# A decoder trunk of two layers: attention as one pipeline of sixteen units, fewer convolution steps in the row split, and another order of the closing sums

## The chip, the cores and the metric

The kernel runs on one core of a Trainium2 chip. The metric is the device time of one execution in microseconds (us), the median of several. The core has these engines, each with its own instruction queue: PE (TensorE, matrix products; PEld is its loading of weights, which overlaps), DVE (VectorE), ACT (ScalarE), POOL (GpSimd) and SP (SyncE, which issues most DMA transfers here). Engines wait for each other through semaphores.

## The reference

512 tokens of width 1024 go through two layers. Layer A has a causal convolution module and a feed-forward network (FFN); then keys and values are projected once; layer B has sliding-window attention over them and another FFN; a last RMSNorm follows.

```python
h = h + conformer_conv(rmsnorm(h, norm_mix[0]), ...)   # pw1 -> GLU -> 31 taps per channel -> LayerNorm -> SiLU -> pw2
h = h + swiglu_ffn(rmsnorm(h, norm_ffn[0]), ffn_w_up[0], ffn_w_down[0])
k, v = split(rmsnorm(h, norm_kv) @ w_kv)               # 4 KV heads of 64
q = rmsnorm(h, norm_mix[1]) @ w_q                      # 16 heads of 64
h = h + banded_sink_attention(q, k, v, sinks, rel_bias) @ w_o
h = h + swiglu_ffn(rmsnorm(h, norm_ffn[1]), ffn_w_up[1], ffn_w_down[1])
out = rmsnorm(h, norm_final)

def banded_sink_attention(...):   # query block n of 128 sees key blocks n-1 and n, window 128
    s = q @ k_band * HEAD_DIM ** -0.5 + bias           # bias by distance; outside the window -1e30
    m = maximum(max(s), sink)
    p = exp(s - m)
    o = p / (sum(p) + exp(sink - m)) @ v_band

def swiglu_ffn(x, w_up, w_down):  # 1024 -> 2 x 2816 -> 1024
    gate, up = split(x @ w_up)
    return (silu(gate) * up) @ w_down
```

## The kernel before

**Layout.** Activations lie transposed: h is eight tiles ("rows" below) of 128 channels by 512 tokens, so each product takes a weight tile of 128x128 and streams tokens past it. Weights come as chunks of 512 KB in a fixed order. For each chunk `get` loads six chunks ahead and splits three ahead into a high part (ACT, L203) and a low part (DVE, L204); a product is then three matmuls in a reduced float32 format: high by high (L262), high by the activation's low part (L263), low by high (L264). Activations are split likewise into pairs (`quad` tiles). Four PSUM banks take one group of output rows.

**Layer A in halves.** The convolution is done for tokens 0 to 255 first (`h0`), then 256 to 511 (`h1`). A tap of the depthwise convolution is one DVE operation (L609, L611), or one ACT product (L601, L603) with a POOL addition (L604); L615 joins the two sums, and L649 is PE's sums over channels for the LayerNorm. The second half's convolution is a generator (`second`) of small steps. `job` gives it points (chunk, steps owed by then), and `pace`, called by every `get`, runs it to the straight line between two points. It runs beside the second pointwise product of the first half (pw2, eight chunks) and the FFN's first part of that half.

**The row split.** After each group of four rows of pw2 the rows of h are added (L731, DVE), scaled by ACT (L382), given their low part by DVE (L383), squared by ACT (L336) and summed by DVE (L340). The FFN's first product takes all eight rows one after the other.

**Attention.** The q product has two groups g of four chunks each. `q_evac` scales a group (L909) and splits it. A unit (gp, jp, n) is four heads of one 128-query block: twelve score matmuls (L928), six each into two banks, whose operands lie in the upper and the lower 64 rows of the array; L931 adds the bias and takes the maximum (DVE, four); exp is L938 (ACT, four); the reciprocal is L940; POOL scales by it (L942, four); L950 transposes on PE; L953 (ACT) and L954 (DVE) split the result into pth and ptl; then come the matmuls with v, and L968 (ACT) and L969 (DVE) split the unit's output. `pipeline(gp)` runs the eight units of a gp, each stage some units apart, in twelve steps. The first one steps beside the chunks of the second q group and is drained before the first o chunk; the second steps beside the first four o chunks and is drained after them. In the first unit of a gp (n = 0, two of eight) the scores are 128 wide in L931, in the others 256.

**The end.** The last FFN part is multiplied out for tokens 0 to 255 (`fa`), then for 256 to 511 (`fb`). Each row of h is added (L1047), squared (ACT, L1051) and the squares of the first five rows of fb (all eight of fa) are summed by POOL (L1053). `total` (L1039) has PE sum over channels; ms (L1070, DVE), rs (L1072, POOL), diag (L1074, DVE) and `spread` (L1084, and L1088 for fb) bring the reciprocal root to all partitions. Then the rows are scaled and stored: six tiles of each half by DVE (L1106), two by ACT and POOL (L1100). `fill` puts DVE products of fa into fb's chain, behind the instruction it names.

What sets the order: the program is written as above, but a scheduler with a timeline model of its own then puts each engine's instructions in order.

Of the kernel before, what the change touches and what calls it, by code (L numbers as in the profile page):

```python
# [21 lines left out]
KT = D // P  # L22
# [127 lines left out]
def hybrid_trunk(ctx: ExitStack, tc: tile.TileContext, xT, W, prm_in, wdw_in, sinks, relb, onehot, outT):  # L150
# [251 lines left out]
        return w == 512 or m % 2 == 1  # L402


    def down_group(keys, act_of, banks, on_step=None):
        nk = len(keys)
        w = banks[0].shape[-1]
        for ci, (key, kts) in enumerate(keys):
            whi, wlo = get(*key)
            order = [(k, m) for k in range(2) for m in range(4)]  # L410
            if ci == nk - 1:
                order = [(k, m) for m in range(4) for k in range(2)]
            for k, m in order:
                sl = slice(m * P, (m + 1) * P)
                mm3(banks[m], (whi[:, k, sl], wlo and wlo[:, k, sl]), act_of(kts + k),
                    ci == 0 and k == 0 and opens(m, w), ci == nk - 1 and k == 1 and closes(m, w))
                if on_step is not None and ci < nk - 1 and m == 3:
                    on_step()
            if on_step is not None and ci == nk - 1:
                on_step()  # L420
                on_step()

# [125 lines left out]
    with tc.tile_pool(name="conv", bufs=2) as cv:  # L548
# [272 lines left out]
            late.gate()  # L821
        h1.after = [h0.silu]
        base = seen[0]
        job(second, (base, 0), (base + 8, 20), (base + 36, h1.n_steps - early))
        x0 = {"ffn0": Act(KT)}
        bc0 = new_bc()
        n0 = Next(("ffn0",), x0, bc0, HALF[0], nc.vector)
# [31 lines left out]
    if True:  # L859
# [42 lines left out]
        qs = [None, None]  # L902
        os_ = [None, None]

        def q_evac(g, banks):
            qs[g] = (quad(), quad())
            for m in range(4):
                t = temp()
                nc.vector.scalar_tensor_tensor(t, banks[m], -HD ** -0.5, rs_bc, op0=ALU.mult, op1=ALU.mult)  # L909
                split((qs[g][0][:, m, :], qs[g][1][:, m, :]), t)  # L910
# [58 lines left out]
            nc.vector.tensor_sub(lo, src, f32(hi))  # L969
            yield  # L970

        def pipeline(gp):
            units = [unit(gp, jp, n) for n in range(NBLK) for jp in range(2)]
            done = 0
            for t in range(len(units) + 4):
                for d in (4, 3, 1, 0):
                    if 0 <= t - d < len(units):
                        next(units[t - d])
                        if d == 1:
                            next(units[t - d])  # L980
                yield

        def drain(it):
            for _ in it:
# [3 lines left out]
        banks = [bank() for _ in range(4)]  # L988
        down_group([(("q", kp, 0), 2 * kp) for kp in range(4)], lambda kt: xq[kt], banks)
        q_evac(0, banks)  # L990
        p0 = pipeline(0)
        banks = [bank() for _ in range(4)]
        down_group([(("q", kp, 1), 2 * kp) for kp in range(4)], lambda kt: xq[kt], banks,
                   on_step=lambda: next(p0, None))
        q_evac(1, banks)
        drain(p0)
        p1 = pipeline(1)
        nxt = Next(("ffn1",))
        for part in range(2):
            for g in range(2):  # L1000
                banks = [bank() for _ in range(4)]
                down_group([(("o", part * 2 + kp, g), 2 * kp) for kp in range(2)],
                           lambda kt: (os_[part][0][:, kt, :], os_[part][1][:, kt, :]), banks,
                           on_step=(lambda: next(p1, None)) if part == 0 else None)
                for m in range(4):
                    i = g * 4 + m
                    nc.vector.tensor_add(h[i], banks[m], h[i])
                    if part == 1:
                        nxt.on_h(i)
            if part == 0:  # L1010
                drain(p1)

    attn.close()
    ffn_part(1, 0, nxt.x["ffn1"], ALL, nxt.rms)
# [5 lines left out]
    class Fin:  # L1020
        def __init__(self, hf):
            self.hf, self.tok = hf, HALF[hf]
            self.banks, self.hg = [bank() for _ in range(4)], []
            self.n_pool = 2

        def down(self, kp, g):
            whi, wlo = get("down", 1, kp, g)
# [14 lines left out]
        def rows(self, g, other=lambda n, ins: None):  # L1042

            n_add = 5 if self.hf else KT
            for i in range(g * 4, g * 4 + 4):
                t = h[i][:, self.tok]
                add = nc.vector.tensor_add(t, self.banks[i // 2][:, (i % 2) * 256:(i % 2) * 256 + 256], t)  # L1047
                if i == KT - 1:
                    other(2, add.ins)
                sq = res.tile([P, 256], F32, tag="sq", name=uid("sq"), bufs=5)  # L1050
                self.squared = nc.scalar.square(sq, t).ins  # L1051
                if 0 < i < n_add:
                    nc.gpsimd.tensor_add(sq, self.acc, sq)  # L1053
                if i < n_add:
                    self.run = self.acc = sq
                if not self.hf or i < n_add:
                    continue
                if i == n_add:
                    self.st = bank()
                self.total(sq, i == n_add, i == KT - 1)  # L1060
                if i == KT - 2:
                    self.total(self.run, False, False)

        def sums(self, other=lambda n, ins: None):
            if not self.hf:
                self.st = bank()
                self.total(self.acc, True, True)
            st = self.st
            ms = small.tile([P, 4], F32, tag="ms", name=uid("ms"))
            other(2, nc.vector.tensor_scalar(ms[:, 0:2], st[:, 0:2], 1.0 / D, EPS, op0=ALU.mult, op1=ALU.add).ins)  # L1070
            rs = small.tile([P, 4], F32, tag="rs", name=uid("rs"))
            nc.gpsimd.tensor_tensor(rs[:, 0:2], ms[:, 0:2], mhalf[:, 0:2], op=ALU.pow)  # L1072
            self.diag = temp()[:, 0:256]
            other(2, nc.vector.tensor_mul(self.diag.rearrange("p (n q) -> p n q", n=2),  # L1074
                                          ident.unsqueeze(1).to_broadcast([P, 2, P]),
                                          rs[:, 0:2].unsqueeze(2).to_broadcast([P, 2, P])).ins)
            for i in range(self.n_pool):
                t = res.tile([P, 256], F32, tag="res", name=uid("res"))
                nc.scalar.mul(t, h[i][:, self.tok], col("fin", i))
                self.hg.append(t)  # L1080

        def spread(self):
            self.pb = bank()[:, 0:256]
            nc.tensor.matmul(self.pb, ones_m, self.diag, start=True, stop=True)  # L1084
            if self.hf:

                pb = bank()[:, 0:256]
                nc.tensor.matmul(pb, ones_m, self.diag, start=True, stop=True)  # L1088
                self.copy(pb)

        def copy(self, pb):
            self.bc = temp()[:, 0:256]
            nc.scalar.copy(self.bc, pb)

        def store(self, i, t, q=nc.sync):
            q.dma_start(outT[i][:, self.tok], t)
# [1 line left out]
        def out_pool(self):  # L1098
            for i, t in enumerate(self.hg):
                nc.gpsimd.tensor_mul(t, t, self.bc)  # L1100
                self.store(i, t, nc.scalar if self.hf else nc.sync)

        def out_dve(self):
            for i in range(self.n_pool, KT):
# [3 lines left out]
                self.store(i, t)  # L1108
                yield

    res = ctx.enter_context(tc.tile_pool(name="res", bufs=8))
    steps = [(kp, g) for kp in range(*LAST) for g in range(2)]
    fa = Fin(0)
    for kp, g in steps:
# [11 lines left out]
    for n, (kp, g) in enumerate(steps):  # L1126
# [5 lines left out]
            fa.spread()  # L1132
        elif n == 3:
            fb.rows(1, fill)
    with tc.issue_after(fb.squared):
        fa.copy(fa.pb)
    fa.out_pool()
    fb.sums(fill)
    fb.spread()
    for _ in fb.out_dve():  # L1140
# [28 lines left out]
```

## Time and profile before

| what | value |
|---|---|
| median of 3 runs | 1115.81 us (1115.38 to 1116.58) |
| the profiled execution | 1115.77 us |
| its span | 1114.0 us |
| mean PE clock | 0.993 of full |
| bytes moved by DMA | 125.00 MB, mean 112 GB/s |
| ACT busy, POOL busy | 502.6 us, 322.1 us |

A row of the timeline has the start, the duration, the engine, the line of the kernel, the operation, output and inputs, and how many instructions it stands for; in brackets follow the idle time before it and what ended that. Matmuls overlap, so what one costs is read from start to start. A row of a group has the total busy time and the mean in ns.

### The profile page before, as it was taken

To read this page: it belongs to the slowest core of one execution; us is meant where nothing else is said; L and a number is where in the kernel's file an instruction comes from. 1 tells how busy PE (TensorE), PEld (TensorE's weight loads), DVE (VectorE), ACT (ScalarE), POOL (GpSimd) and SP (SyncE) were. 2 spreads that over 40 slices of the span, in tenths; PEclk is the share of its full clock that TensorE was granted. 3 is DMA by queue.
4 is the path that set the end of the run, shared out by engine and by line. 5 is a ranking of instruction groups with operands and counts; after the bars stand their busy time and mean duration, and the time that the engine had idled before them with its cause. 6 is when DMAs were issued, how large, how long until landed. Compare 5 with 4: busy or idle time off the path is not lost.

```text
span 1114.0 us, 15803 instructions
## 1 busy us (share of the span) xinstructions
PE 1098.9 (99%) x5994; PEld 955.7 (86%) x5994; DVE 662.3 (59%) x1074; ACT 502.6 (45%) x891; POOL 322.1 (29%) x420
## 2 busy tenths in 40 slices
PE   9999998999999999999999999999999999999997
PEld 8888898999999888888888788888888888888886
DVE  4999999977665454443575686683444333444455
ACT  4786787765543232232343574553322211332233
POOL 4999699700100021110230332241111100110014
PEclk9999998999999999999999999999999999999998
DMA  9227044576655423332322201023233333323332
GB/s 362 100 31 84 25 168 136 183 247 190 189 174 184 135 95 101 105 97 95 95 95 87 75 29 48 30 95 95 95 95 95 97 102 103 96 95 95 95 95 77
DMA packets 40857, 125.00 MB, mean 112 GB/s; under 512 B 4395, under 2 KB 12748, under 8 KB 40780
## 3 DMA queue, kind: packets, MB, share of 16 engines
q1 hardware_dynamic: 40204, 123.55, 36.2%
q8 instruction: 47, 0.77, 0.3%
q10 hardware_dynamic: 576, 0.44, 0.1%
q14 instruction: 30, 0.25, 0.1%
HBM read 118.73 MB, written 5.24 MB: 111 GB/s over the span
## 4 chain that ended last, share of the span: by engine, by line
PE 90%; DVE 5%; ACT 2%; issue 1%; POOL 1%; DMA 0%; SPq 0%; POOLq 0%; DVEq 0%; ACTq 0%
PE bank L263 26%; PE bank L262 26%; PE bank L264 26%; PE bank L562 8%; PE bank L928 1%; DVE quad L383 1%; PE bank L649 1%; ACT pr L603 1%; DVE bank L611 1%; PE bank L950 1%; DVE wlo L204 1%; DMA h<-in_xT_dram 0%; DVE sc L931 0%; PE bank L375 0%; DVE ptl L954 0%
## 5 line engine op out<-in xcount | busy, mean ns | idle before, releaser
L263 PE MATMUL bank<-quad,whi 128*128 128x512 f32 (+1 forms) x1536 | 535.2, 349 | 3.8 <-DVE quad L383 3.7
L262 PE MATMUL bank<-quad,whi 128*128 128x512 f32 (+1 forms) x1536 | 534.8, 350 | 0.5 <-ACT quad L968 0.5
L264 PE MATMUL bank<-quad,wlo 128*128 128x512 f32 (+1 forms) x1536 | 535.1, 348 | 0.0
L204 DVE TENSOR_TENSOR wlo<-raw,whi 128x1024 fp32r<-128x1024 f32 x194 | 262.5, 1354 | 322.4 <-ACT whi L203 312.3
L203 ACT CAST whi<-raw 128x1024 fp32r<-128x1024 f32 x194 | 203.3, 1049 | 360.0 <-PE bank L263 319.3
L263 PEld LDWEIGHTS bank<-quad,whi 128*128 128x128 f32 x1536 | 292.0, 190 | 40.9 <-DVE quad L383 5.0
L262 PEld LDWEIGHTS bank<-quad,whi 128*128 128x128 f32 x1536 | 291.7, 190 | 38.5 <-ACT quad L968 0.9
L264 PEld LDWEIGHTS bank<-quad,wlo 128*128 128x128 f32 x1536 | 292.1, 190 | 36.8 <-issue 0.2
L472 POOL TENSOR_TENSOR tmp<-tmp,tmp 128x512 f32<-128x512 f32 x34 | 48.4, 1425 | 486.7 <-DVE tmp L471 473.1
L604 POOL TENSOR_TENSOR pr<-pr,pr 128x256 f32<-128x256 f32 x208 | 161.6, 825 | 11.0 <-ACT pr L603 11.0
L611 DVE SCALAR_TENSOR_TENSOR bank<-apad,wdw,bank 128x256 f32<-128x256 f32 x248 | 113.2, 485 | 3.6
L562 PE MATMUL bank<-quad,w 128*128 128x256 f32 x512 | 114.2, 382 | 0.6 <-DMA w<-in_W_dram 0.5
L562 PEld LDWEIGHTS bank<-quad,w 128*128 128x128 f32 x512 | 97.4, 191 | 15.4 <-DVE quad L537 1.7
L603 ACT ACTIVATE pr<-apad,wdw 128x256 f32<-128x256 f32 x208 | 99.0, 503 | 20.8 <-POOL pr L604 18.1
L340 POOL TENSOR_TENSOR tmp<-tmp,tmp 128x256 f32<-128x256 f32 (+1 forms) x35 | 38.8, 1109 | 138.6 <-ACT tmp L336 109.1
L470 ACT ACTIVATE tmp<-tmp 128x512 f32<-128x512 f32 x34 | 21.4, 632 | 92.9 <-DVE tmp L469 92.9
L942 POOL TENSOR_SCALAR sc<-sc,sm 128x256 f32<-128x256 f32 (+1 forms) x64 | 30.0, 489 | 79.4 <-DVE sm L940 79.4
L386 ACT CAST quad<-tmp 128x512 fp32r<-128x512 f32 (+1 forms) x50 | 29.1, 586 | 30.4 <-POOL tmp L472 26.6
L471 DVE TENSOR_TENSOR tmp<-bank,rsbc 128x512 f32<-128x512 f32 x34 | 23.5, 691 | 32.4 <-PE bank L264 32.4
L383 DVE SCALAR_TENSOR_TENSOR quad<-h,prm,quad 128x512 fp32r<-128x512 f32 (+1 forms) x40 | 39.5, 1020 | 0.5 <-ACT quad L382 0.4
L938 ACT ACTIVATE sc<-sc,m 128x257 f32<-128x257 f32 (+1 forms) x64 | 30.3, 476 | 15.4 <-DVE m L931 13.7
L387 DVE TENSOR_TENSOR quad<-tmp,quad 128x512 fp32r<-128x512 f32 (+1 forms) x50 | 32.8, 661 | 2.5 <-ACT quad L386 2.5
(140 smaller groups left out, 747.0 us busy)
## 6 DMA issues: line engine op xcount, KB each, us to landing
raw<-in_W_dram SPq DMA_DIRECT2D x202, 512.0 KB, 3.5
w<-in_W_dram SPq DMA_DIRECT2D x15, 512.0 KB, 9.7
fd<-fs SPq DMA_DIRECT2D x1, 3072.0 KB, 33.8
h<-in_xT_dram SPq DMA_DIRECT2D x8, 256.0 KB, 5.9
bias<-fd SPq DMA_DIRECT2D x8, 256.0 KB, 5.5
out_dram<-res SPq DMA_DIRECT2D x14, 128.0 KB, 1.8
w<-in_W_dram SPq DMA_DIRECT2D x2, 256.0 KB, 4.1
out_dram<-res ACTq DMA_DIRECT2D x2, 128.0 KB, 2.7
```

The source lines that it names most:

```text
L203: nc.scalar.copy(hi, r)
L204: lo_engine[0].tensor_sub(lo, r, f32(hi))
L262: nc.tensor.matmul(out, w[0], x[0], start=start, stop=False)
L263: nc.tensor.matmul(out, w[0], x[1], start=False, stop=False)
L264: nc.tensor.matmul(out, w[1], x[0], start=False, stop=stop)
L340: self.eng.tensor_add(sq, self.acc, sq)
L383: nc.vector.scalar_tensor_tensor(dst[1], src, g, f32(dst[0]), op0=ALU.mult, op1=ALU.subtract)
L472: nc.gpsimd.tensor_mul(t2, t1, t2)
L562: mm = nc.tensor.matmul(self.pb[:, w * W2:(w + 1) * W2], w1[ct][:, w, k, :], x[k] if x else xg[k][:, tok], start=k == 0, stop=k == KT - 1)
L603: on_act = nc.scalar.mul(pr, a[:, j:j + W2], tap(j))
L604: on_pool = nc.gpsimd.tensor_add(pr, acc, pr)
L611: on_dve = nc.vector.scalar_tensor_tensor(yt if i == nd - 1 else c, src, tap(i), c if i else self.shift, op0=ALU.mult, op1=ALU.add)
```

## The change

Three edits. First, the points of the convolution job: 17 steps are owed at chunk 6 and 20 at chunk 11 (24.8 by the old line), 47 at chunk 27, and all at chunk 36 as before. Second, `pipeline()` runs all sixteen units in twenty steps. `down_group` calls `on_m(m)` in its last chunk after each finished row m, so that a row of the second q group is scaled and split at once, and steps after every second row; four steps run between the q and the o chunks, and eight beside the first part of o. Third, at the end fa has no tiles for POOL (its eight go through DVE, three for each `fill` instead of two), and in fb the sum of five tiles goes to PE before the square of the seventh row.

```diff
@@ down_group
-    def down_group(keys, act_of, banks, on_step=None):
+    def down_group(keys, act_of, banks, on_step=None, on_m=None):
...
-            if on_step is not None and ci == nk - 1:
+                if on_m is not None and ci == nk - 1 and k == 1:
+                    on_m(m)
+                    if m % 2:
+                        on_step()
+            if on_step is not None and on_m is None and ci == nk - 1:
                 on_step()
                 on_step()
@@ layer A
-        job(second, (base, 0), (base + 8, 20), (base + 36, h1.n_steps - early))
+        job(second, (base, 0), (base + 6, 17), (base + 11, 20), (base + 27, 47), (base + 36, h1.n_steps - early))
@@ attention
-        def q_evac(g, banks):
-            qs[g] = (quad(), quad())
-            for m in range(4):
+        def q_evac(g, banks, ms=range(4)):
+            if qs[g] is None:
+                qs[g] = (quad(), quad())
+            for m in ms:
...
-        def pipeline(gp):
-            units = [unit(gp, jp, n) for n in range(NBLK) for jp in range(2)]
-            done = 0
+        def pipeline():
+            units = [unit(gp, jp, n) for gp in range(2) for n in range(NBLK) for jp in range(2)]
...
-        p0 = pipeline(0)
+        pipe = pipeline()
+
+        def step():
+            next(pipe, None)
+
...
-                   on_step=lambda: next(p0, None))
-        q_evac(1, banks)
-        drain(p0)
-        p1 = pipeline(1)
+                   on_step=step, on_m=lambda m: q_evac(1, banks, [m]))
+        for _ in range(4):
+            step()
...
-                           on_step=(lambda: next(p1, None)) if part == 0 else None)
+                           on_step=step if part == 0 else None)
...
-                drain(p1)
+                drain(pipe)
@@ Fin
-            self.n_pool = 2
+            self.n_pool = 2 * hf
...
-                    other(2, add.ins)
+                    other(3, add.ins)
...
-                self.squared = nc.scalar.square(sq, t).ins
+                nc.scalar.square(sq, t)
...
-                self.total(sq, i == n_add, i == KT - 1)
                 if i == KT - 2:
                     self.total(self.run, False, False)
+                self.total(sq, i == n_add, i == KT - 1)
...
-            other(2, nc.vector.tensor_mul(self.diag.rearrange("p (n q) -> p n q", n=2),
+            other(3, nc.vector.tensor_mul(self.diag.rearrange("p (n q) -> p n q", n=2),
...
-                self.copy(pb)
-
-        def copy(self, pb):
-            self.bc = temp()[:, 0:256]
-            nc.scalar.copy(self.bc, pb)
+                self.bc = temp()[:, 0:256]
+                nc.scalar.copy(self.bc, pb)
...
-                self.store(i, t, nc.scalar if self.hf else nc.sync)
+                self.store(i, t, nc.scalar)
...
-    res = ctx.enter_context(tc.tile_pool(name="res", bufs=8))
+    res = ctx.enter_context(tc.tile_pool(name="res", bufs=16))
...
-    with tc.issue_after(fb.squared):
-        fa.copy(fa.pb)
-    fa.out_pool()
```

How the instructions stand on their engines, at three places. A row has the line, the operation, output and inputs, and the shape; the changed kernel's lines are numbered a few higher (L611 is L615, L928 L933, L950 L955, L1039 L1046, L1084 L1091).

DVE behind the second row split, before:

```order
L383 SCALAR_TENSOR_TENSOR quad_1318<-h,prm,quad_1317 128x256
L340 TENSOR_TENSOR tmp_1618<-tmp_1612,tmp_1618 128x256
L340 TENSOR_TENSOR tmp_1624<-tmp_1618,tmp_1624 128x256
L204 TENSOR_TENSOR wlo_1732<-raw_1573,whi_1731 128x1024
L204 TENSOR_TENSOR wlo_1770<-raw_1633,whi_1769 128x1024
L611 SCALAR_TENSOR_TENSOR bank_1865<-apad_159,wdw,bank_1270 128x256
L611 SCALAR_TENSOR_TENSOR bank_1865<-apad_160,wdw,bank_1270 128x256
L611 SCALAR_TENSOR_TENSOR bank_1865<-apad_159,wdw,bank_1865 128x256
L352 TENSOR_SCALAR ms_1816<-bank_1813 128x2
L204 TENSOR_TENSOR wlo_1828<-raw_1683,whi_1827 128x1024
```

And in the changed kernel:

```order
L383 SCALAR_TENSOR_TENSOR quad_1318<-h,prm,quad_1317 128x256
L340 TENSOR_TENSOR tmp_1610<-tmp_1604,tmp_1610 128x256
L340 TENSOR_TENSOR tmp_1616<-tmp_1610,tmp_1616 128x256
L204 TENSOR_TENSOR wlo_1696<-raw_1573,whi_1695 128x1024
L204 TENSOR_TENSOR wlo_1726<-raw_1625,whi_1725 128x1024
L352 TENSOR_SCALAR ms_1776<-bank_1773 128x2
L204 TENSOR_TENSOR wlo_1788<-raw_1655,whi_1787 128x1024
L204 TENSOR_TENSOR wlo_1834<-raw_1693,whi_1833 128x1024
L615 SCALAR_TENSOR_TENSOR bank_1972<-apad_159,wdw,bank_1270 128x256
L615 SCALAR_TENSOR_TENSOR bank_1972<-apad_160,wdw,bank_1270 128x256
```

Up to the second wlo the two orders are the same, back to the start of the program but for names; behind it three taps of the next channels fell back behind ms and two more wlo.

PE between the last q chunk and the first o chunk (bank_6292 is the output of a unit), before:

```order
L264 MATMUL bank_6210<-pth_6175,vq_5413 128x256
L950 MATMUL bank_6316<-ident,sc_6095 128x128 x4
L263 MATMUL bank_6292<-ptl_6231,vq_5412 128x256
L264 MATMUL bank_6292<-pth_6230,vq_5413 128x256
L262 MATMUL bank_6292<-pth_6230,vq_5412 128x256
L263 MATMUL bank_6292<-ptl_6231,vq_5412 128x256
L264 MATMUL bank_6292<-pth_6230,vq_5413 128x256
L262 MATMUL bank_6292<-pth_6239,vq_5412 128x256
```

And in the changed kernel:

```order
L955 MATMUL bank_6316<-ident,sc_6095 128x128 x4
L933 MATMUL bank_6338<-kq,quad_6128 128x256 x2
L933 MATMUL bank_6338<-kq,quad_6129 128x256
L933 MATMUL bank_6338<-kq,quad_6128 128x256 x2
L933 MATMUL bank_6338<-kq,quad_6129 128x256
L263 MATMUL bank_6292<-ptl_6249,vq_5412 128x256
L264 MATMUL bank_6292<-pth_6248,vq_5413 128x256
L262 MATMUL bank_6292<-pth_6248,vq_5412 128x256
L263 MATMUL bank_6292<-ptl_6249,vq_5412 128x256
L264 MATMUL bank_6292<-pth_6248,vq_5413 128x256
L933 MATMUL bank_6339<-kq,quad_6128 128x256 x2
L933 MATMUL bank_6339<-kq,quad_6129 128x256
```

The scores of the ninth unit now stand between the products of an earlier one, the six of one half of the array apart from the six of the other.

PE at the end, before (sq_9654 is the square of the sixth row, sq_9660 of the seventh, sq_9650 the sum of five, sq_9673 the last):

```order
L264 MATMUL bank_9514<-quad_9073,wlo_9544 128x256
L1084 MATMUL bank_9623<-tmp_9578,ones_m 128x256
L1039 MATMUL bank_9656<-ones_c,sq_9654 128x1 x2
L1039 MATMUL bank_9656<-ones_c,sq_9660 128x1 x2
L1039 MATMUL bank_9656<-ones_c,sq_9650 128x1 x2
L1039 MATMUL bank_9656<-ones_c,sq_9673 128x1 x2
L1084 MATMUL bank_9705<-tmp_9693,ones_m 128x256
```

And in the changed kernel (sq_9650 the sixth, sq_9646 the sum of five, sq_9656 the seventh, sq_9672 the last):

```order
L1091 MATMUL bank_9619<-tmp_9578,ones_m 128x256
L264 MATMUL bank_9514<-quad_9073,wlo_9544 128x256
L1046 MATMUL bank_9652<-ones_c,sq_9650 128x1 x2
L1046 MATMUL bank_9652<-ones_c,sq_9646 128x1 x2
L1046 MATMUL bank_9652<-ones_c,sq_9656 128x1 x2
L1046 MATMUL bank_9652<-ones_c,sq_9672 128x1 x2
L1091 MATMUL bank_9701<-tmp_9686,ones_m 128x256
```

The sum of five moved ahead of the seventh row's square, and the spread of the first half moved ahead of the last product.

## The prediction

> **What bounds the kernel now.** I read the page's span and busy rows first, then the busy time by stretches of 28 us, then the waits of PE, and last the timeline at the three places that the change touches.
>
> ```profile
> span 1114.0 us, 15803 instructions
> PE 1098.9 (99%) x5994; PEld 955.7 (86%) x5994; DVE 662.3 (59%) x1074; ACT 502.6 (45%) x891; POOL 322.1 (29%) x420
> ```
>
> The first number behind an engine is its busy time, the x its instructions. PE is busy for all but 15.1 us of the span, so the end moves only where PE gets work, loses work, runs at a lower clock, or waits. The profiled execution took 1115.77 us, 1.77 more than its span; the median of the three runs shown is 1115.81, so a sum made on the span carries over by adding 1.8.
>
> ```profile
> 168.00:196.00 28.00, 25.75 (x186) 25.20 (x187) 25.59 (x34) 21.66 (x43) 28.00 (x30) 0.88 0.42 136
> 644.00:672.00 28.00, 27.46 (x188) 23.50 (x187) 20.60 (x59) 18.28 (x54) 8.12 (x20) 1.00 0.06 20
> 1092.00:1114.00 22.00, 13.67 (x101) 12.54 (x99) 8.96 (x25) 4.82 (x12) 9.99 (x14) 0.81 0.30 97
> ```
>
> Behind each stretch and its length stand the busy times of PE, weight load, DVE, ACT and POOL, then PE's granted clock, the DMA share and GB/s. These are the stretches in which PE lacks something: the split of the second four rows (2.25 us idle and a clock of 0.88, with POOL busy for all 28 us), the middle of attention (0.54 us idle), and the end. The waits of PE name the producers; the numbers are total us, count, and the longest:
>
> ```profile
> PE bank L263 <- DVE quad L383: 3.7, 3, 1.9
> PE bank L1084 <- DVE tmp L1074: 2.1, 1, 2.1
> PE bank L263 <- DVE ptl L954: 0.8, 2, 0.5
> PE bank L262 <- ACT quad L968: 0.5, 2, 0.3
> ```
>
> These four are what the change can take: 3.7 in the row split, 1.3 in attention, 2.1 at the end.
>
> **Part 1, fewer convolution steps while rows are split.** The first FFN product needs eight rows, each added, scaled by ACT (L382) and given its low part by DVE (L383). PE gets to row 4 and stops:
>
> ```profile
> 169.16 0.39 PE L263 MATMUL bank<-quad,whi 128*128 128x256 f32 x1 [1.88 <-DVE quad L383]
> 171.20:177.40 6.20, 6.11 (x28) 0.50 0.00 0
> 177.40:179.20 1.80, 1.80 (x17) 1.00 0.59 164
> 156.55 26.37 POOL L604 TENSOR_TENSOR pr<-pr,pr 128x256 f32<-128x256 f32 x26
> L383 DVE SCALAR_TENSOR_TENSOR quad<-h,prm,quad 128x256 fp32r<-128x256 f32 x4 | 2.5, 637 | 0.4 <-ACT quad L382 0.4
> L383 DVE SCALAR_TENSOR_TENSOR quad<-h,prm,quad 128x256 fp32r<-128x256 f32 x4 | 3.7, 946 | 0.0
> ```
>
> The second and third rows are PE in two windows: 28 matmuls in 6.20 us at clock 0.50 (0.221 each), then 17 in 1.80 at full clock (0.106 each). So the place costs 3.7 us of waiting and 28 x (0.221 - 0.106) = 3.2 us of slow clock, 6.9 in all. The last two rows are L383 by shape in the first split (144 to 153 us, 637 ns) and the second (167 to 176 us, 946 ns).
>
> The new points owe 20 steps at the eleventh chunk where the old ones owe 24.8, and both owe all 65 at chunk 36. But the scheduler sets the order: on DVE and ACT it is the same instruction for instruction through the four L383 of the second split, and POOL is fed the same adds; only what follows the split on DVE moves. POOL's 26 adds run without a gap across it. So I take it that the rows come when they came, and the stall stays. On PE four sums (L649) move from ahead of the chunk to just before the stop, time-neutral, and six matmuls instead of four stand between the waits for rows 4 and 5, so two fewer are left behind the last: 2 x 0.221 = 0.4 at most, 0.2 at full clock. I take **-0.3**. Bounds: nothing, and -6.9 if stall and slow clock both go. The steps put off come before chunk 36, and the half they build is not needed until the FFN of the first half is through.
>
> The Trainium skill, "TensorE: Matmul & The Clock Gate", section "What's actually happening", has the clock fall to half after an idle window of about 3.4 us, in windows that run freely. By the longest gap here, 1.88 us, there would be no drop; the 0.50 says that shorter gaps suffice, so by the rule 3.2 us would not be there, and by the row they are.
>
> **Part 2, one pipeline of sixteen units.** The number of matmuls is the same. Three things change: where the drain between the q and the o chunks stood, scores of four later units now stand; how the scores of a unit lie among the other matmuls; and on which engine the stage leans.
>
> *Scores.* Six of a unit's twelve L928 matmuls go to each row half of the array.
>
> ```profile
> 648.17 0.97 PE L928 MATMUL bank<-kq,quad 64*128 64x256 f32 x6
> 649.07 0.39 PE L263 MATMUL bank<-ptl,vq 128*128 128x256 f32 x1
> 696.82 0.98 PE L928 MATMUL bank<-kq,quad 64*128 64x256 f32 x12
> 697.73 0.50 PE L264 MATMUL bank<-quad,wlo 128*128 128x512 f32 x1
> 704.47 1.32 PE L928 MATMUL bank<-kq,quad 64*128 64x256 f32 x12
> 705.72 0.39 PE L262 MATMUL bank<-pth,vq 128*128 128x256 f32 x1
> ```
>
> Start to start, twelve that alternate between the halves take 0.91 us, six of one half by themselves 0.90, and twelve that go half after half 1.25. A unit broken into two runs by half therefore costs 0.89 more, half after half 0.34 more. By the order, units broken so go from three and one broken in three (put at 1.1, a switch more than two) to six; half after half from one to two; the mixed rest stays within 0.3. Before: 3 x 0.89 + 1.1 + 0.34 + 0.5 = 4.6; after: 6 x 0.89 + 0.68 + 0.2 = 6.2. That is **+1.6**, since PE waits for nothing at most of these places; 0 where a run fills a wait.
>
> *Stalls.* The waits on ptl and on the attention output cost more than their idle time, since the pipe runs empty:
>
> ```profile
> 657.03 0.38 PE L262 MATMUL bank<-pth,vq 128*128 128x256 f32 x1
> 657.76 0.39 PE L263 MATMUL bank<-ptl,vq 128*128 128x256 f32 x1 [0.34 <-DVE ptl L954]
> 657.99 0.28 PE L264 MATMUL bank<-pth,vq 128*128 128x256 f32 x1
> 658.11 0.28 PE L262 MATMUL bank<-pth,vq 128*128 128x256 f32 x1
> 656.00:660.00 4.00, 3.66 (x29) 3.25 (x28) 3.30 (x10) 3.19 (x9) 3.35 (x9) 1.00 0.01 2
> 660.00:664.00 4.00, 3.94 (x30) 3.51 (x29) 2.42 (x5) 2.32 (x6) 0.81 (x4) 1.00 0.00 0
> 617.19 0.35 DVE L931 CUSTOM_DVE_ANT_0 sc<-bank,bias,sk 128x128 f32<-128x128 f32 x1 [0.59 <-PE bank L928]
> 624.96 0.48 DVE L931 CUSTOM_DVE_ANT_0 sc<-bank,bias,sk 128x256 f32<-128x256 f32 x1 [0.49 <-PE bank L928]
> ```
>
> From 657.03 to 657.76 it is 0.73 us where the next pair takes 0.12: 0.61 lost for 0.34 shown, 0.27 more. Four such stops: 1.3 + 4 x 0.27 = 2.4 us, two at each drain. With other work between, and the last steps spread over the o chunks, three of the four should go (-1.8); the last unit has nothing behind it and keeps its own. Against that DVE gets the score passes (L931) of four units in this stage, eight of 128 and eight of 256 columns: 8 x 0.35 + 8 x 0.48 = 6.6 us of records, some 5.4 without their overlap. In the eight microseconds after 656 it was idle 0.70 + 1.58 = 2.3 us, and PE's own stage grows by the scores of the four units, two of them broken, one alternating, one half after half: 2 x 1.80 + 0.91 + 1.25 = 5.8 us. It just fits. I put a stop of the same kind, 0.4, there: **-1.4** net. Bounds: -2.4, and +1.5 if DVE's excess (5.4 - 2.3 = 3.1) delays PE by half. Part 2 is thus +0.2, between -2.4 and +3.1.
>
> **Part 3, the end.**
>
> ```profile
> 1101.17 0.59 PE L1084 MATMUL bank<-tmp,ones_m 128*128 128x256 f32 x2
> 1101.60 0.50 PE L1039 MATMUL bank<-ones_c,sq 128*128 128x1 f32 x4
> 1101.36 0.76 DVE L1047 TENSOR_TENSOR h<-bank,h 128x256 f32<-128x256 f32 x2 [0.68 <-PE bank L264]
> 1102.35 1.50 PE L1039 MATMUL bank<-ones_c,sq 128*128 128x1 f32 x12 [0.26 <-ACT sq L1051]
> 1103.89 0.16 DVE L1070 TENSOR_SCALAR ms<-bank 128x2 f32<-128x2 f32 x1 [0.99 <-PE bank L1039]
> 1103.97 0.86 DVE L1106 SCALAR_TENSOR_TENSOR res<-h,prm,bank 128x256 f32<-128x256 f32 x2
> 1105.49 0.43 DVE L1074 TENSOR_TENSOR tmp<-ident,rs 128x256 f32<-128x256 f32 x1 [0.66 <-POOL rs L1072]
> 1103.38 1.41 POOL L1100 TENSOR_TENSOR res<-res,tmp 128x256 f32<-128x256 f32 x2 [1.40 <-ACT tmp L1093]
> 1104.75 0.71 POOL L1072 TENSOR_TENSOR rs<-ms,mhalf 128x2 f32<-128x2 f32 x1
> ```
>
> Today rs stands ready at 1103.97 but waits on POOL behind two products (1103.38 to 1104.75), 0.78 us. They go to DVE, as two more L1106 of 0.43. A total is four matmuls, 1.50 / 3 = 0.5: with the five-tile sum ahead of the sixth square, that 0.5 leaves the last chain. Against it the first half's spread now stands ahead of the last product on PE (0.43 for its two passes, 1101.17 to 1101.60 by the start of the first total), which delays the last add. DVE: ms about 0.1 to 0.3 earlier, at 1103.7; three products instead of two behind it (1.3) end at 1105.0, while rs ends at 1104.4. So diag starts at 1105.0 to 1105.2 for 1105.49: **-0.4**. Bounds: -0.8 (all that rs waited) and +0.5 (the spread's delay with nothing won). The stores after that are as many as before.
>
> Sum: -0.3 + 0.2 - 0.4 = -0.5, span 1113.5, time **1115.3**.
>
> **The rivals.** *Faster: the split is relieved after all.* If adds on POOL thin out, L383 falls to the 637 ns of the first split: 4 x 0.31 = 1.2 us, and with shorter gaps the 3.2 us of slow clock can vanish: -4.4, 1111.3. For it: L383's two durations with the same shape, and that the gap decides a drop; against it: the unchanged orders of DVE, ACT and POOL. The Trainium skill, "SBUF — State Buffer", section "SBUF: two separate sides", has a DVE operation with two SBUF inputs and a GpSimd operation lock each other out; 946 against 637 ns agree with it, but POOL is busy in both splits.
>
> *Slower: DVE becomes the pacer between q and o.* If the four units' score passes come ahead of ptl (L954) and the output's low part in DVE's queue, every inserted unit stops PE: none of the 1.8 is saved, +1.6 for broken scores, +1.5 for the delay, -0.7 for parts 1 and 3: +2.4, 1118.2. It decides once DVE's 5.4 us exceed its 2.3 idle plus what PE's stage grows; DVE's 3.30 of 4 us in the first window speaks for it, 2.42 in the second against it.
>
> *The scheduler undoes it:* each term lands at its zero end, 1115.8; this belongs to the first forecast.
>
> **How the numbers follow.** About 0.2% (2.2 us) is what can be told from no change, so "same" is 1113.6 to 1118.0. My forecast has 0.53: its terms' ordinary spread gives 1113.0 to 1117.5, of which 0.08 falls to faster, 0.41 to same, 0.04 to slower. The relieved split has 0.25, all faster. DVE as pacer has 0.22: 0.18 slower, 0.04 same. Faster 0.33, same 0.45, slower 0.22. The range takes in the relieved split's middle and the pacer's: 1111.7 to 1118.4.
>
> **What would show it.** Right: PE's wait on L383 stays near 3.7 us with clock 0.50 for about 6 us behind it; score rows of x6 in six units; no stop on ptl before the first o matmul and one at the end; rs directly behind ms, its diag 0.3 to 0.5 us earlier against the end. Wrong: a clock of 1.00 through that split, or waits on L383 under 2 us; new waits of PE on ptl or on the attention output above 2 us in all; DVE without a gap between q and o.

## The result, and the profile after

| | before | changed |
|---|---|---|
| median of 21 runs | 1115.90 us | 1116.74 us |
| lowest, highest | 1115.01, 1119.36 us | 1115.98, 1119.16 us |
| ratio | | 1.0011, 95% interval 1.0005 to 1.0016 |
| span of the profiled execution | 1114.0 us | 1116.6 us |

The changed kernel is slower by 0.11%, some 1.2 us by the ratio and 0.8 between the medians. Its runs spread more than those of before: 10 of the 21 lie above 1117.5 us, where one of before does. The page of the profiled execution, its busy row and the waits of PE (dots stand for two at the start of the program, on `ones_m` and on the first weights, which are there before as well):

```profile
span 1116.6 us, 15805 instructions
PE 1099.2 (98%) x5994; PEld 956.5 (86%) x5994; DVE 664.0 (59%) x1076; ACT 500.4 (45%) x888; POOL 320.3 (29%) x418
```

```profile
PE bank L263 <- DVE quad L383: 3.9, 4, 1.2
PE bank L566 <- DVE quad L541: 2.0, 1, 2.0
PE bank L1091 <- DVE tmp L1081: 1.5, 1, 1.5
PE bank L264 <- DVE wlo L204: 1.3, 1, 1.3
...
PE bank L1046 <- POOL sq L1060: 0.5, 1, 0.5
...
PE bank L262 <- ACT whi L203: 0.4, 1, 0.4
```

Against the four waits of before: the one on L383 is still there (3.9 for 3.7, in four pieces instead of three), the two of attention are gone from the list, the one at the end is 1.5 for 2.1, but the wait on a square ahead of it is 0.5 (on POOL) where it was 0.3 (on ACT). New are three: on L541, on wlo and on whi. The first stands at the start of the program, where nothing was changed:

```profile
7.91 0.79 PE L566 MATMUL bank<-quad,w 128*128 128x256 f32 x1 [2.00 <-DVE quad L541]
```

There DVE waits for the second transfer of the input; a second profile of the same kernel (below) does not have it, so these 2.0 us of the 2.6 by which the spans differ belong to that execution. The other two are at one chunk of weights:

```profile
205.39 0.39 PE L262 MATMUL bank<-quad,whi 128*128 128x256 f32 x1 [0.42 <-ACT whi L203]
207.24 0.39 PE L264 MATMUL bank<-quad,wlo 128*128 128x256 f32 x1 [1.35 <-DVE wlo L204]
```

PE needs the high part 0.42 us before ACT has it, and two matmuls later the low part 1.35 us before DVE has it. Nothing in the kernel before waits there.

To set one kernel beside another I added up, for all of PE's rows in a stretch, the time from one start to the next less the usual spacing of that shape: what PE lost there by waiting, by a slow clock and by switching. This is worked out from the timelines; the stretches are the row split (160 to 182 us), the stage behind it (182 to 232) and the second half's pw2 (232 to 300).

| kernel (profiled execution) | split | behind | pw2 | sum |
|---|---|---|---|---|
| before | 6.6 | 0.1 | 0.5 | 7.2 |
| changed | 5.3 | 2.9 | 0.4 | 8.6 |
| changed, second profile | 5.8 | 2.6 | 0.5 | 8.9 |
| only the points changed | 4.0 | 5.8 | 0.5 | 10.3 |
| only attention and end changed | 6.2 | 0.0 | 0.3 | 6.5 |

Each row is one execution, and a kernel's executions differ by 3 us and more: the second profile, at 1116.14 us, is the fastest of 11 whose median is 1117.91. So the table shows where time goes, and the medians below how much. The split did become cheaper, by 0.8 to 2.6 us, and the stage behind it took back more.

### The profile page after: what moved, and what is told of

Its sections match the earlier page's. It is cut to its first block, busy times and chain, and to the rows that moved or that the text cites. A ratio compares the mean times of both kernels' runs of the same rounds, so it can differ in the third digit from the quotient of the medians.

```text
span 1116.6 us, 15805 instructions
## 1 busy us (share of the span) xinstructions
PE 1099.2 (98%) x5994; PEld 956.5 (86%) x5994; DVE 664.0 (59%) x1076; ACT 500.4 (45%) x888; POOL 320.3 (29%) x418
## 4 chain that ended last, share of the span: by engine, by line
PE 88%; issue 3%; ACT 3%; DVE 3%; POOL 2%; DMA 1%; SPq 0%; POOLq 0%; ACTq 0%
PE bank L262 25%; PE bank L263 25%; PE bank L264 25%; PE bank L566 8%; PE bank L933 2%; POOL pr L608 2%; ACT pr L607 1%; PE bank L955 1%; PE bank L653 1%; DVE quad L383 1%; DMA h<-in_xT_dram 1%; DVE bank L615 0%; DVE wlo L204 0%; ACT whi L203 0%; ACT quad L382 0%
## 5 line engine op out<-in xcount | busy, mean ns | idle before, releaser
L615 DVE SCALAR_TENSOR_TENSOR bank<-apad,wdw,bank 128x256 f32<-128x256 f32 x248 | 113.3, 485 | 3.6
L383 DVE SCALAR_TENSOR_TENSOR quad<-h,prm,quad 128x512 fp32r<-128x512 f32 (+1 forms) x40 | 39.5, 1021 | 0.5 <-ACT quad L382 0.4
```

What stands on the lines that cost most here:

```text
L383: nc.vector.scalar_tensor_tensor(dst[1], src, g, f32(dst[0]), op0=ALU.mult, op1=ALU.subtract)
L615: on_dve = nc.vector.scalar_tensor_tensor(yt if i == nd - 1 else c, src, tap(i), c if i else self.shift, op0=ALU.mult, op1=ALU.add)
```

## The experiments

### Each part alone

Two kernels have one part of the diff each with the old points (attention; end), one has the points alone, and one has attention and end together.

```diff
-        job(second, (base, 0), (base + 8, 20), (base + 36, h1.n_steps - early))
+        job(second, (base, 0), (base + 6, 17), (base + 11, 20), (base + 27, 47), (base + 36, h1.n_steps - early))
```

> Only the points of the convolution job are changed. Theory A (the points cost: the steps put off past chunk 11 crowd ACT, whose cast of a weight chunk, L203, then stands behind convolution products that wait for POOL, so PE waits near 205 us): about +1.6 us against before, and PE waits on whi and on wlo of 1.5 to 2 us in all between 195 and 215 us. Theory B (the points cost nothing, the slower time is the late input transfer at the start of the profiled run or the attention): within 0.5 us of before and no PE wait on whi or wlo there.

> Only the attention is one pipeline of sixteen units. Theory A: about -1.1 us, by what the two traces show between the last FFN product of layer A and the first of layer B; no PE wait on ptl or on the attention output in the middle. Theory B: +0.5 to +2.5 us, as broken score runs cost more than the stops saved.

> Only the end is changed. Theory A: -0.1 to 0 us, by the two traces. My prediction's term: -0.4 us, with the wait of PE on diag at 1.5 for 2.1 us and the last add 0.43 us later.

> The changed kernel with the old points of the convolution job. Theory A: -1.0 to -1.3 us against before, and some 1.6 us less than the changed kernel, with no wait on whi or wlo near 205 us. Theory B: +0.8 us, as the changed kernel.

| kernel | median | before, same chip | ratio, 95% interval |
|---|---|---|---|
| points alone | 1118.01 | 1116.20 | 1.0017 (1.0008 to 1.0025) |
| attention alone | 1115.05 | 1116.20 | 0.9989 (0.9980 to 0.9997) |
| end alone | 1115.99 | 1116.20 | 1.0001 (0.9992 to 1.0010) |
| attention and end | 1114.99 | 1116.20 | 0.9990 (0.9981 to 0.9999) |

The parts add up: 1.9 - 1.2 + 0.1 = +0.8 us, for +1.2 measured. The points cost, the attention gains, the end does nothing; without the points the change is a gain. The timeline of the kernel with the points alone shows where:

```profile
185.56 0.70 PE L375 MATMUL bank<-tmp,ones_m 128*128 128x256 f32 x2 [1.54 <-ACT tmp L362]
203.33 0.38 PE L262 MATMUL bank<-quad,whi 128*128 128x256 f32 x1 [0.41 <-ACT whi L203]
205.18 0.38 PE L264 MATMUL bank<-quad,wlo 128*128 128x256 f32 x1 [1.35 <-DVE wlo L204]
```

Two stops behind the split: the spread of the root waits for its diagonal, then the same late chunk.

### The same kernel once more

> The changed kernel once more, for a second profile and as the measure of the next three on one chip. Theory A (the time lost behind the row split is there in every run; the late input transfer of the first profile is an event of that run): +0.8 to +1.8 us against before, PE waits on whi and wlo near 203 us of about 1.8 us, and a wait on the diagonal (L362) near 185 us if PE's clock held in the split. Rival (the first profile was an odd one): no such waits.

1117.91 us against 1115.90 of before on that chip, ratio 1.0015 (1.0007 to 1.0024). The profile, of an execution of 1116.14 us, has no late input, and the waits at the late chunk are those of the first profile: 0.41 at 203.18, 1.35 at 205.03. So the chunk is late, to a tenth of a microsecond alike, in all three profiles in which only the points or the whole change differ from before. ACT and then DVE ahead of it, in the second profile:

```profile
196.67 0.51 ACT L607 ACTIVATE pr<-apad,wdw 128x256 f32<-128x256 f32 x1 [1.12 <-POOL pr L608]
197.08 1.03 ACT L203 CAST whi<-raw 128x1024 fp32r<-128x1024 f32 x1
198.13 1.28 ACT L467 ACT_TABLE_LOAD   x1
199.43 0.63 ACT L467 ACTIVATE tmp<-tmp 128x512 f32<-128x512 f32 x1
...
200.89 1.29 ACT L607 ACTIVATE pr<-apad,wdw 128x256 f32<-128x256 f32 x3
202.09 1.03 ACT L203 CAST whi<-raw 128x1024 fp32r<-128x1024 f32 x1
```

```profile
201.62 1.00 DVE L615 SCALAR_TENSOR_TENSOR bank<-apad,wdw,bank 128x256 f32<-128x256 f32 x2
203.16 1.82 DVE L204 TENSOR_TENSOR wlo<-raw,whi 128x1024 fp32r<-128x1024 f32 x1 [0.53 <-ACT whi L203]
```

The two casts start 5.0 us apart without a gap on ACT: between them lie a function table, SiLU and products of the convolution, and ahead of the first ACT waits for POOL. The second cast ends at 203.1, 0.4 us after PE stood ready; DVE's part of it ends 1.9 us later.

But ACT is not much later than before. The same chunk in the kernel before, where nothing waits: ACT and DVE, then PE's first product with it and, ahead of that, the last row of a group of sums for the convolution's LayerNorm.

```profile
196.12 1.03 ACT L203 CAST whi<-raw 128x1024 fp32r<-128x1024 f32 x1
...
201.41 1.03 ACT L203 CAST whi<-raw 128x1024 fp32r<-128x1024 f32 x1
202.48 1.79 DVE L204 TENSOR_TENSOR wlo<-raw,whi 128x1024 fp32r<-128x1024 f32 x1 [0.58 <-ACT whi L203]
```

```profile
198.67 0.59 PE L649 MATMUL bank<-sq,ones_m 128*128 128x256 f32 x2
...
204.86 0.28 PE L262 MATMUL bank<-quad,whi 128*128 128x256 f32 x1
```

The two casts start 5.3 us apart there, with the same table load between them, and the second ends only 0.7 us earlier than in the changed kernel. What moved is PE: it is ready for the chunk at 202.6 instead of 204.9. The split lost 0.8 us less, and a group of eight sums (1.7 us), which before runs from 197 to 199 us, stands behind the chunk with the new points:

```profile
207.76 0.59 PE L653 MATMUL bank<-y,ones_m 128*128 128x256 f32 x2
```

So the steps that were held back took this group of sums out from in front of the chunk, and PE waits where it used to work.

### Is it ACT?

The function table of SiLU is loaded early, where ACT idles; once in the changed kernel, once with the old points.

```diff
             late.gate()
+        with tc.issue_after(late.sig):
+            nc.scalar.activation(warm, warm, AF.Silu)
         h1.after = [h0.silu]
```

> The changed kernel, with the function table of SiLU loaded on ACT right after the last sigmoid of the gates, where ACT idles, rather than 1.28 us long in the middle of the casts near 200 us. Theory A (ACT is what PE waits for at 203 to 208 us: the cast of a weight chunk stands behind the table load and the convolution products): the waits on whi and wlo there fall from 1.8 us by up to 1.3 us, and the time by 1 to 1.5 us against the changed kernel, to 1115.3 to 1115.8. Rival (POOL paces ACT there, so a table load more or less is absorbed, or PE waits for DVE's own queue): within 0.4 us of the changed kernel, 1116.4 to 1117.

> The same early table load with attention and end changed but the old points of the convolution job. Theory A: PE has no wait on a cast there, so nothing changes against that kernel: 1114.7 to 1115.3. If the table load held up something else as well, it falls below 1114.5.

The changed kernel with it: 1116.50 us against 1116.64 of before on that chip, ratio 1.0000 (0.9991 to 1.0009), so about 1 us better than the change by the ratios, though their intervals overlap; the wait on wlo at the late chunk is 0.64 us for 1.35, that on whi is gone, but its profile has a stop of the spread, 2.11 us, as the kernel with the points alone has. With the old points: 0.9991 (0.9982 to 1.0000), as without the early table. That agrees with ACT being what PE waits for behind the split under the new points, and under the old ones not; since the intervals overlap, it does not show it.

The second way to lighten ACT and POOL left out three of the 31 taps in two channel tiles, in the changed kernel and in before:

```diff
                 nd = TAPS - n_pool
+                if self.hf == 1 and ct // 2 == 1:
+                    n_pool -= 3
```

> The changed kernel without three of the 31 taps in two channel tiles of the second half's convolution (the second pair, on ACT and POOL alone: six products and six additions less between 180 and 213 us). Theory A: casts come up to 3 us earlier, the waits on whi and wlo go, and the time falls by 1.8 to 2.5 us, to about 1114.5. Rival (the loss lies in the order of PE, or in the clock alone): within 0.5 us of the changed kernel.

> The kernel before, without the same three taps. Theory A: no wait on a cast there, so no change: within 0.4 us of before. Rival (the conv work itself slows this stage): as much faster as the changed kernel without them, 1.5 us or more.

Neither reading came out: 1.0005 (0.9996 to 1.0014) and 1.0010 (1.0001 to 1.0020). Before without the taps is slower though it has less to do. The scheduler had put PE's and ACT's instructions in another order, and the late chunk was then an earlier one (waits of 0.74 on whi and 1.31 on wlo at 200 to 202 us). The pair tells nothing about taps.

### Is it the place of single instructions on PE?

With the new points a group of sums (L649) that stood at 160 us, ahead of the first FFN chunk, stands behind that chunk, the next one behind the late chunk (above), and the spread 13 matmuls earlier. One kernel holds the spread back, one asks for the sums three steps earlier, one has the early table too.

```diff
-                    due += [(4, lambda p=p: self.squares(p)), (8, lambda p=p: self.sums(p))]
+                    due += [(4, lambda p=p: self.squares(p)), (5, lambda p=p: self.sums(p))]
```

> The changed kernel with the spread of the first half's root (L375 on PE) held back behind the chunk that it stood in the middle of, 17 matmuls later. Theory A: the wait on L362 near 185 us goes (up to 1.5 us); PE then comes earlier to the late cast near 203 us and gives back what it gained there: the waits on whi and wlo grow by as much, and the time falls by 0.5 us at most. Rival (the two stops are separate losses): 1 to 1.5 us less than the changed kernel.

> The changed kernel with the channel sums of the second half's convolution (L649) asked for three steps earlier: on PE the second group stands 48 matmuls further ahead, in front of the late cast again, the first in front of the chunk, and the spread nine matmuls later. Theory A (the new points moved 1.7 us of PE work from in front of the late casts to behind them): 1 us less than the changed kernel or more, waits on whi and wlo under 0.8 us. Rival (the casts themselves come too late, whatever PE does): no change beyond 0.3 us.

> The changed kernel with both, the early table load and the earlier sums. Theory A: the stop near 203 us is gone and the split keeps what it gained: 1.5 to 2.5 us less than the changed kernel, as fast as the kernel with old points (1115.0) or faster. Rival: no better than the early table load alone.

The spread held back: 1116.37 us, 1.0005 (0.9997 to 1.0014), 1.5 us less than the same chip's changed kernel. The sums earlier: 1118.06, 1.0026 (1.0014 to 1.0039); with the table as well 1118.06, 1.0027 (1.0015 to 1.0038). Their waits of PE, in that order, one row or two of each:

```profile
PE bank L262 <- ACT rsbc L370: 2.0, 1, 2.0
```

```profile
PE bank L263 <- DVE quad L383: 4.9, 4, 1.8
PE bank L653 <- DVE y L642: 1.0, 1, 1.0
```

```profile
PE bank L653 <- DVE y L642: 5.3, 2, 4.3
```

In all three the waits at the late chunk are gone, and in all three PE stops elsewhere: for the copy of the root, for the rows of the split, for a row that the convolution's sums need. That the late chunk's waits go was expected of the last two; of the first the opposite was, and its gain of 1.5 us between the medians is what the rival said, though the intervals overlap. The sums of the three stretches are 8.6, 7.9 and 7.8 us, for 8.6 to 8.9 of the change, but the last two also stop ahead of 160 us, where the change does not: for 1.2 and 5.6 us. My theory that the place of the sums on PE costs the time fell here as a whole: putting them back took away the stop at the late chunk, moved the loss and did not lower it.

### Holding back, or catching up?

All four have the new attention and end.

```diff
e13  (base, 0), (base + 6, 17), (base + 11, 20), (base + 36, all)
e14  (base, 0), (base + 8, 20), (base + 11, 22), (base + 36, all)
e15  (base, 0), (base + 8, 20), (base + 11, 25), (base + 27, 52), (base + 36, all)
e16  (base, 0), (base + 8, 24), (base + 36, all)
```

> Attention and end changed, points (0, 0), (6, 17), (11, 20), (36, all): steps held back between chunks 6 and 11 as in the change, but caught up evenly. Theory H (holding back costs): 1 to 2 us slower than the kernel with the old points, that is -0.2 to +0.8 us against before, with stops of PE behind the split. Theory C (the fast catch-up costs): -1.2 us against before, as with the old points.

> The same with points (0, 0), (8, 20), (11, 22), (36, all): a hold of half the depth; the sums of the first pair stay in front of the chunk. Theory H: between, -0.8 to -0.2 us against before. If the place of the sums on PE decides and not the steps, -1.2 us.

> The same with points (0, 0), (8, 20), (11, 25), (27, 52), (36, all): no hold, but steps as fast between chunks 11 and 27 as in the change. Theory H: -1.2 us against before, no stop behind the split. Theory C: -0.2 us or slower, with waits on whi and wlo near 203 us.

> The same with points (0, 0), (8, 24), (36, all): four steps more ahead of and in the split. Theory H in its strong form (the later the steps the worse): -1.2 us or better against before. Rival (the split is loaded by them, which is what the points were moved for): a longer wait on L383 and -0.5 us or slower.

| points | median | before, same chip | ratio, 95% interval | lost: split, behind, pw2 |
|---|---|---|---|---|
| hold to chunk 11, even after | 1118.37 | 1116.21 | 1.0016 (1.0007 to 1.0026) | 5.4, 3.6, 2.1 |
| mild hold | 1118.85 | 1116.21 | 1.0018 (1.0007 to 1.0029) | 8.5, 1.2, 3.7 |
| no hold, fast after | 1115.06 | 1116.21 | 0.9985 (0.9977 to 0.9994) | 4.9, 1.8, 0.5 |
| four steps more early | 1116.92 | 1116.21 | 1.0006 (0.9997 to 1.0014) | 6.5, 2.0, 0.5 |

The hold costs, and the fast catch-up does not: by the ratios, steps held back and caught up evenly are 1.8 us slower than before, steps that are only caught up fast 1.7 us faster, and the intervals lie apart. How much a hold costs does not follow its depth. The mild one was expected between the two, and it is as slow as the full one, +2.0 us. Its loss is not behind the split either: it has a wait of 3.6 us on L383 in the split, and most of the rest at the convolution's end (its profile is the slowest of its executions, 1120.92 us, that of the kernel without a hold the fastest, 1114.39). Both held kernels pay where the convolution ends: PE stops near 232 us at the sums of its LayerNorm or right behind them, for ACT's copy of them. The first one's wait there:

```profile
PE bank L662 <- ACT tmp L659: 1.7, 1, 1.7
```

The strong form of the theory, that earlier is always better, fell with the last kernel: four steps more load the split, where PE waits 4.9 us in five pieces.

What the hold does to DVE is read from windows. Those from 176 to 192 us and from 204 to 224 us, with busy PE, PEld, DVE, ACT and POOL in that order; before, then the changed kernel's second profile, then the kernel without a hold:

```profile
176.00:192.00 16.00, 16.00 (x130) 15.95 (x129) 13.82 (x20) 11.96 (x24) 16.00 (x17) 0.96 0.49 164
204.00:224.00 20.00, 20.00 (x169) 20.00 (x168) 19.96 (x30) 13.63 (x21) 11.88 (x11) 1.00 0.61 189
```

```profile
176.00:192.00 16.00, 16.00 (x130) 15.95 (x130) 11.03 (x14) 12.17 (x24) 16.00 (x17) 0.97 0.55 165
204.00:224.00 20.00, 18.97 (x151) 18.76 (x152) 19.96 (x30) 12.88 (x19) 8.46 (x8) 1.00 0.61 185
```

```profile
176.00:192.00 16.00, 15.51 (x128) 15.25 (x128) 13.81 (x20) 11.95 (x24) 16.00 (x17) 1.00 0.52 164
204.00:224.00 20.00, 19.91 (x156) 18.87 (x154) 19.96 (x30) 13.64 (x20) 11.77 (x11) 1.00 0.63 194
```

Right behind the split DVE waits for casts that stand on ACT behind products that wait for POOL. Before, taps fill these gaps: 13.8 of 16 us. With the hold it does 11.0; 2.8 us of taps are left over. From 204 us on DVE is full in all three (19.96 of 20 us), so the taps that were put off come where there is no room, and the convolution's last sums start 7.5 us later in the changed kernel (232.5 for 225.0). But PE does not wait for them there: behind the late chunk it loses no more than before up to 300 us. That the taps left over on DVE are what makes the hold cost is thus argued, not shown; no run moved them alone.

## Why the prediction was wrong

**The step that failed** is the price of the held-back convolution in part 1. The prediction had it at -0.3 and said of the steps: "The steps put off come before chunk 36, and the half they build is not needed until the FFN of the first half is through." That names the last reader of the work, not the engine that has to do it. The points cost +1.9 us alone, 5.8 us lost behind the split for 0.1. What the traces show in place of the -0.3 is that the held steps took a group of sums out from in front of a chunk of weights, so that PE came to that chunk 2.2 us earlier, while its cast came 0.7 us later: 1.8 us of waits. The prediction followed one group of sums, calls its move time-neutral, and did not look at the next, nor at how busy DVE and ACT are behind the split, though the order of DVE there is quoted ahead of it. Why other holds lose as much at other places stays open.

Term by term it is +1.9 for -0.3, -1.2 for +0.2 and +0.1 for -0.4. That the total is only 1.4 us off is luck: the misses of +2.2 and -1.4 half cancel.

**That the stall stays** was right: the wait on L383 is 3.9 us (3.1 in the second profile) for 3.7, and the orders through the split are what decided that. **That the relieved split is a rival** was half right. Its slow clock did go in one profile, that of the points alone (1.00 from 166 to 184 us); but PE, early by that, came to a diagonal, a cast and a low part that were not early. (Its price of -4.4 gives 1111.4, not 1111.3.) Neither rival had this: a gain in the split that the queue behind it takes back. 4.0 us lost in the split instead of 6.6, and 5.8 behind it instead of 0.1, is the points alone in one row.

**The attention** was forecast at +0.2 and measured at -1.2 (alone; the timelines give -1.1). The broken scores cost what was said: start to start they take 20.6 us for 18.9, +1.7 for +1.6. The stops were mis-sized: the matmuls with v take 23.1 us for 26.3, -3.1 for -1.4. Some 2.0 of it are the large stops (2.3 before, 0.4 after; 1.8 was forecast), the stop of 0.4 that I added between q and o did not come, and the other 1.1 are short gaps between the matmuls with v, which I had not counted. The transposes take 0.4 more, which makes -1.1 in all. The slower rival, DVE as pacer, did not come true; its 5.4 us fitted into the idle time and the longer stage. The same windows as in the prediction, of the changed kernel; its stage starts 4.0 us later in this execution (649.8 for 645.8 us), so its second window stands against the first of before:

```profile
656.00:660.00 4.00, 4.00 (x30) 3.60 (x31) 4.00 (x15) 2.89 (x11) 2.44 (x5) 1.00 0.27 92
660.00:664.00 4.00, 4.00 (x30) 3.43 (x29) 3.12 (x16) 3.58 (x14) 3.07 (x8) 1.00 0.01 2
```

PE has no idle time in either, where it had 0.34 and 0.06. DVE is full in the first, as it is before four microseconds earlier, and has 0.9 us to spare in the second.

**The end** was forecast at -0.4 and is nothing. The changed kernel there:

```profile
1105.46 1.58 PE L1046 MATMUL bank<-ones_c,sq 128*128 128x1 f32 x12 [0.52 <-POOL sq L1060]
1107.08 0.16 DVE L1077 TENSOR_SCALAR ms<-bank 128x2 f32<-128x2 f32 x1 [0.50 <-PE bank L1046]
1107.31 0.71 POOL L1079 TENSOR_TENSOR rs<-ms,mhalf 128x2 f32<-128x2 f32 x1 [1.91 <-DVE ms L1077]
1108.06 0.43 DVE L1081 TENSOR_TENSOR tmp<-ident,rs 128x256 f32<-128x256 f32 x1
```

POOL takes rs at once, as forecast. But the sum of five, which PE now takes ahead of the seventh row's square (the prediction says the sixth), is not there yet: POOL's last addition to it sets PE's wait of 0.52, so the three totals still run behind it. With the spread ahead of the last product that eats up the gain. From the start of the last product's last matmul to diag it was 4.44 us (1101.05 to 1105.49) and is 3.92 (1104.14 to 1108.06), with 0.5 of spread now in front of it.

## What to carry to other kernels

Work that is put off to relieve one place has to be paid where it lands: look at each engine that does it, PE with its small sums too, in the stretch where it will come and in the one that it leaves, and not only at who needs the result. Where several queues feed PE in turn, a stop that goes shows the next one behind it; the time of the whole stage, not of the stop, is what to watch, and a gap that a filler used is a cost when the filler moves. Make the parts of a change separable and run each alone: here a gain of 1.2 us lay under a loss of 1.9. Attention and end with the old points, or with the old ones and a fast catch-up, beat both kernels (0.9990 and 0.9985 of before; their intervals overlap, so which is better is open).

## What was not expected of the hardware

The same pauses of PE made the clock fall in one execution and not in another. The points alone and the second profile of the change have the same order on PE there and waits that begin alike (1.15 and 0.76 us; 1.17 and 0.76 us). Two windows of the first, then one of the second, PE alone with its clock:

```profile
172.00:178.20 6.20, 5.20 (x43) 1.00 0.06 18
206.00:209.20 3.20, 3.20 (x17) 0.50 0.61 169
```

```profile
172.00:178.20 6.20, 5.87 (x33) 0.61 0.12 22
```

In one execution the clock held in the split and fell behind the stop at 203 us, in the other it fell in the split and held there. The Trainium skill, "TensorE: Matmul & The Clock Gate", section "What's actually happening", has windows of about 3.4 us that run freely; two executions that differ at like pauses fit that. It has the clock fall after an idle window; in the second execution the pauses were 1.17 and 0.76 us with matmuls between them, so here a window with pauses was enough. That the wide spread of the changed kernel's runs comes from this was not measured: each profile shows one execution.
